# The input projection of a hybrid decoder layer as a stage of its own in seven-product form, with the scan as one chain behind it

## The chip, the cores and the metric

The kernel runs on one core of one Trainium2 chip. Its engines are PE (TensorE, matmul, with its weight loads listed as PEld), DVE (VectorE), ACT (ScalarE), POOL (GpSimd) and SP (SyncE, which here issues nearly all DMAs). The metric is the time of one execution in device microseconds; the profile records another execution, instruction by instruction.

## What is computed

One layer of a decoder on 1024 prompt tokens and 8 x 8 sample tokens, width 1024, in fp32. Cut to what matters here:

```python
x = x + 0.5 * swiglu(rmsnorm(x, norm_ffn1), ffn1_w_in, ffn1_w_out)      # D_FF = 2816
hn = rmsnorm(x, norm_mix)
proj = hn @ w_in                      # 1024 -> 8224: u 1024, z 2048, xbc 3072, dt 32, gates 2048
branch_pool = pool_mix(u) @ pool_w_out     # windowed means (2, 4, 8, 16) minus token, a 256x256 map per group
xbc_c = silu(causal_conv(xbc, width 4))    # x 2048, B 512, C 512
dt = softplus(dt_raw + dt_bias)
y = ssd_scan(x, dt, A, B, C, state) + d_skip * x       # 32 heads of 64, 4 groups, state 128, chunks of 128
y = rmsnorm_per_group(y * silu(z)) * ssd_norm
branch_ssd = y @ ssd_w_out
merged = sigmoid(g0) * branch_pool + sigmoid(g1) * branch_ssd
x = x + merged @ w_o
x = x + 0.5 * swiglu(rmsnorm(x, norm_ffn2), ffn2_w_in, ffn2_w_out)
```

The last rows before pooling and convolution and the last scan states are outputs too.

## The kernel before

The tokens stand in the free dimension, features in the partitions. They are worked in two halves: half 0 has 512 prompt tokens, half 1 the other 512 and the 64 sample tokens (`NTOK = (512, 576)`). A matmul in fp32 accuracy is three matmuls of a fast fp32 type: every operand is split into a high part (ACT) and the remainder (DVE), and `products` (L318) runs high x high, low x high, high x low. `dense` (L329) makes one output tile of 128 features for one half: 8 blocks of 128 inputs x 3 products, in half 1 as two pieces of 288 columns. `load_w` (L269) fetches a block of weights, splits it on ACT (`wh`, L292) and DVE (`wl`, L293) and, with `keep`, writes both parts to DRAM, so that half 1 reads them back instead of splitting again.

FFN1 and FFN2 use another form (`wino`, L481): the 2 x 2 block product of two token quarters, two input quarters and two output tiles is done in seven block products in place of eight. `combine` (L508) makes the sums of the activations, `wino_weights` (L442) the sums of the weights on POOL (L451) and their splits (L457, L458), and a callback `after` gathers the products from three PSUM banks. Both halves of the tokens are worked on with one loading of the weights. A few leading tiles are done in the plain form (`ffn_in_plain`) while the sums for the other half are made.

Between the FFNs stands the token mixer, `mix_half` (L1375), once for each half. It runs `mix_dt` (step sizes), `mix_pool` (u tiles, windowed sums, group map, `gate` and `pool_w_out`, L962 to L1062), then, for each of four groups, `proj_group` (L1094: six `conv_tile`s: projection `pc`, convolution on DVE at L1088, SiLU by tanh), `z_tiles` (L1381), the group's scan `ssd_group` (L1323), the gating (L1355) and `ssd_out` (L1392, `pso`), then the merge and `w_o` (`pwo`).

The scan of a group goes chunk by chunk, 4 chunks of 128 tokens and in half 1 a fifth for the samples. A chunk has a first part `ssd_a` (L1168: transposes `pxT`, `pcb`, scaled inputs, decays), a second part `ssd_b` (L1224: `pyo`, `pyd`, additions into `y4`; for the samples also the states of eight sequences, `ph0T`, `pnew`, `pyos`) and the state step `ssd_st` (L1302: `pst`, `hst`). The second part of a chunk comes after the first part of the next. The gating multiplies by z (L1359), squares, sums (`rstd`, L367, with `pss`, a power on POOL at L361, `prb`), scales and splits into `yh`, `yl` (L1364 to L1370).

What runs beside what is written by a planner in the kernel. Side work stands in `Chain`s, generators that yield a delay; the clock `pe` counts the columns of the matmuls issued so far, and after each step of a dense matmul `tick` runs the chains whose time is due. `finish` steps one chain to its end at once, whatever its due times. So instructions of the scan stand between dense matmuls in PE's order when there are such matmuls, and next to each other when a `finish` forces them. Each engine then works its own order one after the other.

Of the kernel before, what the change touches and what calls it, by code (L numbers as in the profile page):

```python
# [38 lines left out]
N_PLAIN, N_APART = (3, 2), 1  # L39

PRODUCTS = (("1", 0), ("2", 1), ("6", 0), ("5", 2), ("7", 0), ("3", 2), ("4", 0))

STEP = (6.5, 4.8)
SSD0 = (2.0, 2.0)
CONV_D = (1.0, 3.0)
STEP_S = 2.5
GP = (0.7, 1.2)
PACE = 2.0
# [9 lines left out]
PART_AT, PART_W, PART_PACE = 20.0, 4.0, 3.0  # L58
N_PRE = 3
# [3 lines left out]
def tile_hybrid_pool_ssd_macaron(  # L63
# [45 lines left out]
    def fx(dt=F32, name="x"):  # L109
        if stage["name"] == "mix":  # L110
            return act((P, 576), dt, name)
        return stage["p"].tile([P, 576], dt, tag="fx", bufs=N_FX, name=nm(name))
# [104 lines left out]
    cwh = cp.tile([P, 5, 24], F32, tag="cwh", name="cwh")  # L217
# [13 lines left out]
    def load_consts():  # L231
# [16 lines left out]
        for j in range(4):  # L248
            V.tensor_scalar_mul(cwh[:, j, :], cols[:, i_cw[j] : i_cw[j] + 24], 0.5)
        V.tensor_scalar_mul(cwh[:, 4, :], cols[:, i_cb : i_cb + 24], 0.5)  # L250
# [9 lines left out]
    dtd_sd = dp.tile([NS, NH], F32, tag="dtdsd", name="dtdsd")  # L260

# [105 lines left out]
    def rstd(tiles, h, count, out, pace=1.0):  # L367
# [4 lines left out]
        for i, x in enumerate(tiles):  # L372
            if i == 0:
                S.activation(s, x, AF.Square)
            else:
                q = act((P, N), name="sq")
                S.activation(q, x, AF.Square)
                V.tensor_tensor(s, s, q, op=ALU.add)
# [27 lines left out]

    def norm_split(xt, h, gi, out, pace=1.0):

        N = NTOK[h]
        rr = []  # L410
        yield from rstd(xt, h, D, rr, pace)
        hi, lo = [], []
        for k in range(KD):
            a, b, _ = pair(N)
            t = act((P, N), name="xn")
            V.tensor_tensor(t, xt[k], rr[0], op=ALU.mult)
            split(t, a, b, cols[:, gi + k : gi + k + 1])
            hi.append(a)
            lo.append(b)
            yield pace  # L420
        out.append((h, hi, lo))
# [217 lines left out]
    def ffn(wi, wo, prep, after, half=None, side=None):  # L639

        X, todo, behind = [{}, {}], [], []
        for h in HALVES:
# [11 lines left out]
            for ff in range(N_PLAIN[h]):  # L656
                ffn_in_plain(wi, ff, x[:3])
            todo.append(c)
            behind.append(start(rest(c, gen)))
        for c in behind:  # L660
            finish(c)
        if side:
# [133 lines left out]
    def norm_parts(xt, h, gi, out, pace=1.0):  # L796
# [5 lines left out]
        for k in range(KD):  # L802
            x = fx(name="xn") if k >= 4 else act((P, 576), name="xn")
# [6 lines left out]
            hl.append(both)  # L810
            yield pace
        out.append((h, hi, lo, xn, hl))


    ch, hn = {}, []
    wi1 = ffn1_w_in[0]

    def after1(h, xt):
        if h == 0:
            ch["hn"] = start(norm_split([t[:, : NTOK[0]] for t in xt], 0, i_gm, hn, HN_PACE), HN_AT)  # L820
        for m in range(KD):
            dma(xspill[h][m], xt[m][:, : NTOK[h]])

# [20 lines left out]
    def side():  # L844
        yield from part(ffn1_w_out[0], out01)
        yield from part(ffn2_w_in[0], [(kb, 4, c0 + ff * P) for ff in range(N_PLAIN[0]) for kb in (0, 4) for c0 in (0, FF)])
        yield from part(w_o[0], [(kb, 4, m * P) for m in range(KD) for kb in (0, 4)])

    ffn(wi1, ffn1_w_out[0], prep1, after1, side=side())
    finish(ch["hn"])  # L850
# [4 lines left out]
    W = w_in[0]  # L855
    uhist = cp.tile([P, KD, HIST], F32, tag="uhist", name="uhist")
    chist = cp.tile([P, 24, 3], F32, tag="chist", name="chist")
# [11 lines left out]
    def evac_raw(pts, h, raw, off, raws, offs):  # L869

        if h == 0:
            S.copy(raw[:, off : off + 512], pts[0][:, :512])
            return
        S.copy(raw[:, off : off + 288], pts[0][:, :288])
        S.copy(raw[:, off + 288 : off + 512], pts[1][:, :224])
        S.copy(raws[:, :, offs : offs + NT], pts[1][:, 224:288].rearrange("p (b t) -> p b t", t=NT))

    def mix_dt(h, xs, out):

        N = NTOK[h]  # L880
        nch = 4 + h
        n = nch * NH
# [729 lines left out]
```

## Time and profile before

| | us |
|---|---|
| median of 3 runs (lowest, highest) | 2930.04 (2925.57, 2930.72) |
| the profiled execution | 2926.27 |
| its span, first to last instruction | 2924.5 |
| granted clock of PE in it | 0.998 |
| start and end of the token mixer in it | 790, about 2165 |

The prediction shows lines of several views: the page (busy time by engine, the span in 40 slices, shares of the chain that ended last), groups of instructions (`line engine operation out<-in shapes xcount | busy us, mean ns of one | idle time of the engine before them, and what ended it`), the chain in order of time and the timeline (`start us, us, what`), and stretches (`from:to length, busy us (xinstructions)` of PE, PEld, DVE, ACT, POOL, then the granted clock, the share of the DMA engines and GB/s).

### The profile page before, as it was taken

The numbers are of one execution on the slowest core, as the hardware profiler recorded it, in microseconds if no ns is written. First come the engines' busy times: TensorE is split into PE (matmuls) and PEld (weight loads), VectorE is DVE, ScalarE is ACT, GpSimd is POOL, SyncE is SP. The second block draws the span as 40 slices with busy tenths as digits, with TensorE's granted clock in tenths as the row PEclk, the third lists the DMA queues.
The fourth block names the chain that finished last, engine by engine and source line by source line (L and its number), as shares of the span: only waits on it lengthen the run. The fifth ranks groups of instructions, "written<-read, shape, count | busy, mean of one in ns | idle before, by whom it ended". The sixth has DMA issues, their size and how long they took to land.

```text
span 2924.5 us, 50164 instructions
## 1 busy us (share of the span) xinstructions
PE 2873.3 (98%) x18622; PEld 2621.2 (90%) x18622; DVE 1706.2 (58%) x3172; ACT 1208.9 (41%) x2456; POOL 533.3 (18%) x642
## 2 busy tenths in 40 slices
PE   7999999999999999999999999999999999999998
PEld 6999999789988888788999989999999999987898
DVE  6665555434273897787643786867666554453432
ACT  5444444323242655443332554443233444443422
POOL 6444444000000000000000010100035444440000
PEclk9999999999999999999999999999999999999999
DMA  4575554854335878678434566556574532236652
GB/s 135 166 227 181 161 173 131 283 188 145 101 97 164 281 254 265 205 226 280 129 98 148 170 187 185 168 165 186 177 244 154 162 98 78 82 103 210 216 161 73
DMA packets 542266, 501.23 MB, mean 171 GB/s; under 512 B 36388, under 2 KB 391780, under 8 KB 542014
## 3 DMA queue, kind: packets, MB, share of 16 engines
q1 hardware_dynamic: 542006, 498.03, 54.4%
q8 instruction: 146, 2.39, 0.3%
q14 instruction: 98, 0.80, 0.1%
q10 hardware_dynamic: 16, 0.00, 0.0%
HBM read 355.94 MB, written 142.20 MB: 170 GB/s over the span
## 4 chain that ended last, share of the span: by engine, by line
PE 90%; DMA 4%; DVE 3%; ACT 1%; issue 1%; POOL 1%; SPq 0%; POOLq 0%; ACTq 0%; DVEq 0%
PE pw L164 26%; PE po L164 18%; PE pc L164 9%; PE pg L164 8%; PE pz L164 7%; PE pu L164 5%; PE pso L164 5%; PE pbp L164 3%; PE pwo L164 3%; PE pyd L164 1%; PE pst L164 1%; PE pyo L164 1%; DMA bsel<-in_bsel_dram 1%; PE pgm L164 1%; DMA hr<-hd 1%
## 5 line engine op out<-in xcount | busy, mean ns | idle before, releaser
L293 DVE TENSOR_TENSOR wl<-wraw,wh 128x512 fp32r<-128x512 f32 (+1 forms) x416 | 284.4, 685 | 409.2 <-ACT wh L292 396.0
L292 ACT ACTIVATE wh<-wraw 128x512 fp32r<-128x512 f32 (+1 forms) x416 | 257.4, 620 | 617.6 <-PE po L164 248.7
L164 PE MATMUL pw<-X,wh 128*128 128x288 f32 (+1 forms) x1416 | 353.9, 329 | 5.3 <-ACT v L574 3.5
L164 PE MATMUL pw<-X,wl 128*128 128x288 f32 (+1 forms) x936 | 268.6, 287 | 0.0
L164 PEld LDWEIGHTS pw<-X,wh 128*128 128x128 f32 x1416 | 237.6, 188 | 27.3 <-ACT v L574 4.2
L164 PE MATMUL pc<-hl,wh 128*128 128x288 f32 (+1 forms) x1152 | 256.6, 331 | 0.0
L164 PE MATMUL pw<-hl,wh 128*128 128x512 f32 x608 | 219.5, 396 | 1.1 <-DVE t L578 1.0
L458 DVE TENSOR_TENSOR wl<-s,wh 128x512 fp32r<-128x512 f32 x168 | 131.9, 785 | 144.4 <-ACT wh L457 122.8
L164 PE MATMUL po<-hh,wh 128*128 128x288 f32 (+1 forms) x800 | 210.4, 323 | 3.5 <-ACT hh L353 2.5
L164 PE MATMUL po<-hr,wh 128*128 128x288 f32 (+1 forms) x800 | 210.6, 322 | 0.1
L164 PE MATMUL po<-hh,wl 128*128 128x288 f32 (+1 forms) x800 | 210.0, 322 | 0.0
L164 PE MATMUL pg<-hl,wh 128*128 128x288 f32 (+1 forms) x864 | 201.7, 338 | 0.8 <-issue 0.8
L164 PEld LDWEIGHTS pc<-hl,wh 128*128 128x128 f32 x1152 | 184.5, 188 | 18.1 <-issue 3.5
L164 PE MATMUL pw<-hi,wh 128*128 128x288 f32 x640 | 189.1, 296 | 0.6 <-ACT t L610 0.6
L164 PE MATMUL pw<-hi,wl 128*128 128x288 f32 x640 | 188.4, 294 | 0.0
L164 PE MATMUL pw<-lo,wh 128*128 128x288 f32 x640 | 188.4, 294 | 0.0
L164 PEld LDWEIGHTS pw<-X,wl 128*128 128x128 f32 x936 | 176.5, 189 | 0.0
L164 PE MATMUL pz<-hl,wh 128*128 128x288 f32 (+1 forms) x768 | 174.4, 335 | 0.0
L164 PE MATMUL pw<-hl,wl 128*128 128x256 f32 x608 | 169.2, 278 | 0.0
L164 PE MATMUL pc<-hl,wl 128*128 128x288 f32 (+1 forms) x576 | 158.2, 328 | 0.0
L164 PEld LDWEIGHTS pg<-hl,wh 128*128 128x128 f32 x864 | 141.3, 189 | 15.7 <-issue 2.5
L458 DVE TENSOR_TENSOR wl<-wraw,wh 128x512 fp32r<-128x512 f32 x126 | 103.2, 819 | 87.5 <-ACT wh L457 81.0
(375 smaller groups left out, 6872.7 us busy)
## 6 DMA issues: line engine op xcount, KB each, us to landing
wh<-part SPq DMA_DIRECT2D x204, 256.0 KB
wl<-part SPq DMA_DIRECT2D x204, 256.0 KB
wraw<-in_ffn_w_in_dram SPq DMA_DIRECT2D x188, 256.0 KB
wraw<-in_w_in_dram SPq DMA_DIRECT2D x180, 256.0 KB
wraw<-in_ffn_w_out_dram SPq DMA_DIRECT2D x120, 256.0 KB
part<-wh SPq DMA_DIRECT2D x112, 256.0 KB
part<-wl SPq DMA_DIRECT2D x112, 256.0 KB
ab<-acsd SPq DMA_DIRECT2D x64, 256.0 KB
```

The costliest lines, as they stand in the source:

```text
L164: T.matmul(out, lhsT, rhs, start=start, stop=stop, skip_group_check=free)
L292: S.activation(wh, raw, AF.Copy)
L293: V.tensor_tensor(wl, raw, wh.bitcast(F32), op=ALU.subtract)
L458: V.tensor_tensor(wl, a, wh.bitcast(F32), op=ALU.subtract)
```

## The change

The input projection becomes a stage between FFN1 and the mixer, `in_proj`. The norm of both halves is made as for an FFN (`norm_parts`, `operands` with `combine`); the dt tile, 6 gate tiles of half 0 and 4 of half 1 are done in plain form, and everything else in pairs of output tiles, `proj_pair`, in seven-product form for both halves at once. Each finished tile goes to a work list from which a chain, `worker`, takes convolution and SiLU (`post_conv`), windowed sums and the difference (`post_u`), SiLU of z and tanh of the gates. All results go to DRAM (`convd`, `zd`, `gd`, `dhd` and `dld`, `dtp`).

```diff
+    def proj_pair(kind, ia, ib, xs):
+        while len(work) > 3:
+            poster[0].step()
...
+        wino(wino_weights(W, 0, 4, 4, c0 + ia * P, c0 + ib * P), 4, xs, after)
...
+    def in_proj(prep):
+        def plain(x):
+            dts.append(mix_dt(h, [x]))
+            for i in range(N_GATE[h]):          # (6, 4)
+                pg = dense(W, 0, KD, OFF_G0 + i * P, [x], name="pg0")[0]
...
+        for i in range(N_GATE[0], 16, 2):
+            proj_pair("g", i, i + 1, both)
+        for g in range(NG):
+            for kind, ia, ib in (("c", 16 + g, 20 + g), ("c", 4 * g, 4 * g + 1), ("c", 4 * g + 2, 4 * g + 3),
+                                 ("u", 2 * g, 2 * g + 1), ("z", 4 * g, 4 * g + 1), ("z", 4 * g + 2, 4 * g + 3)):
+                proj_pair(kind, ia, ib, both)
...
+        for i in range(N_GATE[1], N_GATE[0], 2):
+            proj_pair("g", i, i + 1, both[1:])
```

```diff
+    def post_conv(h, ct, raw, new):
+        for o, f in parts:
+            S.activation(o, f(0), AF.Identity, bias=..., scale=w[0])
+        yield POST
+        for j in range(1, 4):
+            for o, f in parts:
+                V.scalar_tensor_tensor(o, f(j), w[j], o, op0=ALU.mult, op1=ALU.add)
+            yield POST
+        S.activation(t[:, :N], t[:, :N], AF.Silu)
+        dma(convd[h][ct], t[:, :N])
```

The mixer keeps what follows the projection: `pool_branch` for both halves (group map and `pool_w_out`), then for each half `ssd_out` for the groups, `merge` and `out_proj`. The scans of all eight groups of both halves are one chain, `scan`, started at the head of the mixer, which reads a group's inputs back from DRAM one group ahead; the step between its parts is 7.0 on the planner's clock (6.5 and 4.8 before). `ssd_out` steps the chain on until its group is there and finishes the group's gating.

```diff
+    def scan():
+        for i, (h, g) in enumerate(todo):
+            nxt = fetch(*todo[i + 1]) if i + 1 < len(todo) else None
+            yield from ssd_group(h, g, *cur, dts[h])
+            yn = []
+            gated[h, g] = start(gating(h, g, cur[2], yn)), yn
+            cur = nxt
+
+    cs = start(scan())
+
+    def scanned(h, g):
+        while (h, g) not in gated:
+            cs.step()
+        finish(gated[h, g][0])
+        return gated[h, g][1][0]
...
+    for h in HALVES:
+        pool_branch(h)
+    for h in HALVES:
+        acc = [None] * KD
+        for g in range(NG - 1):
+            ssd_out(h, g, acc)
+        mhl = merge(h, acc)
...
+        x1 = out_proj(h, *mhl)
```

Within the scan and the gating, work moves from ACT and DVE to POOL: the skip product (ACT before, at L1326, for a whole group; now per chunk and in place), the last addition into the group's result (L1300), the product with z and the sums of squares. z is read from DRAM at the head of the gating.

```diff
+        G.tensor_tensor(xs4[:, :, tok], xs4[:, :, tok], Dcol[...], op=ALU.mult)
...
-            V.tensor_tensor(ysl, ysl, ea, op=ALU.add)
+            G.tensor_tensor(ysl, ysl, ea, op=ALU.add)
...
-    def gating(h, g, y4, z4, out):
+    def gating(h, g, y4, out):
+        E = V if (h, g) == (1, NG - 1) else G
+        zs = []
         for j in range(4):
-            V.scalar_tensor_tensor(y4[:, j, :N], z4[j], 0.5, y4[:, j, :N], op0=ALU.mult, op1=ALU.mult)
+            z = act((P, N), name="z")
+            dma(z, zd[h][g * 4 + j])
+            zs.append(z)
...
+        for j in range(4):
+            E.tensor_tensor(y4[:, j, :N], y4[:, j, :N], zs[j], op=ALU.mult)
...
-        yield from rstd([y4[:, j, :N] for j in range(4)], h, 512, rr, GP[0])
+        yield from rstd([y4[:, j, :N] for j in range(4)], h, 512, rr, GP[0], E)
+        while h * NG + g - 2 >= freed[0]:
+            yield 1.0
```

Smaller parts: the weights of `pool_w_out` are split ahead during FFN1, as those of `w_o` were; in the projection no weights are kept in DRAM any more, since they are loaded once for both halves; the states before pooling and convolution are written out tile pair by tile pair.

More of the change, by code (lines that the diff above doesn't have):

```diff
@@ L637, in ffn_in_plain, with operands @@
         dma(hdram[h][ff], g[:, : NTOK[h]])
[L639 to L643 removed]
+    def operands(prep, plain):
+        X, behind = [{}, {}], []
         for h in HALVES:
```

784 lines of the change are left out of this document (417 added, 367 removed).

## The prediction

> **What bounds the kernel now.** First the page: busy shares, the 40 slices, the chain that ended last.
>
> ```profile
> span 2924.5 us, 50164 instructions
> PE 2873.3 (98%) x18622; PEld 2621.2 (90%) x18622; DVE 1706.2 (58%) x3172; ACT 1208.9 (41%) x2456; POOL 533.3 (18%) x642
> ...
> PE   7999999999999999999999999999999999999998
> ...
> DVE  6665555434273897787643786867666554453432
> ...
> PE 90%; DMA 4%; DVE 3%; ACT 1%; issue 1%; POOL 1%; SPq 0%; POOLq 0%; ACTq 0%; DVEq 0%
> ```
>
> TensorE (PE) is the bound nearly everywhere, so a matmul removed is worth its own length as long as another stands ready behind it. The token mixer runs from 790 to about 2165 us; the stretches by half, and one stretch of FFN1 in seven-product form, are the next view (busy us of PE, PEld, DVE, ACT, POOL; clock; DMA share; GB/s):
>
> ```profile
> 790.20:1399.10 608.90, 607.62 (x2948) 496.73 (x2949) 438.52 (x812) 287.95 (x517) 19.23 (x59) 1.00 0.70 221
> 1399.10:2165.00 765.90, 761.26 (x6020) 733.84 (x6019) 498.22 (x1120) 300.54 (x663) 52.51 (x117) 1.00 0.55 167
> ...
> 365.00:438.00 73.00, 73.00 (x491) 68.62 (x490) 42.00 (x67) 33.72 (x70) 33.04 (x32) 1.00 0.53 171
> ```
>
> In the mixer PE stands still for 1.3 + 4.6 = 6 us in all: the scan, a chain over VectorE (DVE), ScalarE (ACT) and PE, is hidden behind projection matmuls that stand between its pieces. That cover is what the change takes away.
>
> **Part 1: projection matmuls.** The chain in order of time gives the plain prices, 24 matmuls a tile in half 0, 48 in half 1:
>
> ```profile
> 906.26 5.44 PE pbp L164 x24
> 911.70 5.44 PE pg L164 x24
> ...
> 1531.77 6.40 PE pg L164 x48
> ```
>
> The projection has 64 tiles (24 convolution, 16 z, 8 u, 16 gate) and the small dt tile. Plain remain dt, 6 gate tiles of half 0 and 4 of half 1. Removed: 58 x 5.44 + 60 x 6.40 = 699.5 us. Added: 29 pairs for both halves, each 7 products x (8 + 12) = 140 matmuls, and one pair for half 1 alone, 84. FFN1 has the same 140: 73.00 / 491 = 0.149 us each, 20.8 a pair. 29 x 20.8 + 84 x 6.40/48 = 614. **Saving 85 us**; the transposes of the states are the same in number. The weights no longer kept and reloaded and the results through DRAM are off PE; DMA is busy 0.70 and 0.55 above, so I cost them at nothing (uncovered they would show as waits for `wraw`). The norm of half 1 runs behind the seven plain tiles of half 0, 7 x 5.44 = 38 us, SiLU takes the place of tanh and a product: nothing either.
>
> **Part 2: DVE in the new stage.**
>
> ```profile
> L1088 DVE SCALAR_TENSOR_TENSOR ct<-craw,cwh,ct 128x512 f32<-128x512 f32 x144 | 107.6, 747 | 32.3 <-ACT ct L1086 31.2
> L1088 DVE SCALAR_TENSOR_TENSOR ct<-crs,cwh,ct 128x64 f32<-128x64 f32 x72 | 20.0, 278 | 0.0
> L293 DVE TENSOR_TENSOR wl<-wraw,wh 128x512 fp32r<-128x512 f32 x250 | 171.9, 688 | 166.2 <-ACT wh L292 164.2 <-PE prb L168 0.8 <-DMA ab<-acsd 0.7
> L458 DVE TENSOR_TENSOR wl<-s,wh 128x512 fp32r<-128x512 f32 x68 | 55.1, 810 | 51.4 <-ACT wh L457 48.8 <-POOL s L451 1.5 <-issue 0.5
> L578 DVE TENSOR_TENSOR t<-pw,t 128x512 f32<-128x512 f32 x18 | 12.3, 684 | 0.2
> L614 DVE TENSOR_TENSOR g<-pw,t 128x288 f32<-128x288 f32 x17 | 7.7, 452 | 6.6 <-PE pw L164 6.6
> ```
>
> A convolution pair holds 12 wide steps (9.0 us), 6 sample steps (1.7), 7 weight remainders (5.7) and seven additions from PSUM (3 x 0.68, one half as wide at an estimated 0.4, 3 x 0.45: 3.8): 20.2 of the 20.8 us that PE needs. The z pairs have only the last two (9.5), so the stage fits on average, but half of its pairs are full, and the work list lets three items lag, no more. A stall of 0 at the least; at most, some 3 us for each of 12 convolution and 4 u pairs, 48. I take 12, near the lower end, because FFN1 with the same bank rhythm has PE at 73.00 of 73.00.
>
> **Part 3: the scan without its cover.** After the change the dense work beside the scan is `pbp` and `pwo`, 16 x (5.44 + 6.40) = 189 us, as much again for `pso`, and the small `pgm`; the pool branch's part of it runs before the first `pso`, and a group's `pso` can't start before its scan and gating are done. The built order of PE shows what that leaves. From the last `pso` of one group of half 1 to the first of the next nothing dense stands there:
>
> ```
> pso:48 | pyo pyd pst pxT pcb | pyo pyd pst pxT pcb | pyo pyd pst pxT pcb px3 pb3 px3 pb3 | pyo pyd
> | 8 x (ph0T pnew) with 2 x (pyos pyT) | pyd pfin | pss prb pss | pxT pcb | pso:90 ...
> ```
>
> This stands so for (1,1), (1,2) and (1,3), from the sample's ph0T on for (1,0), from the second chunk on for (0,3), and for the last chunk's tail and the gating for (0,2). There the scan runs at the pace of DVE:
>
> ```profile
> L1218 DVE TENSOR_SCALAR ab<-ab,acs 128x128 f32<-128x128 f32 x256 | 55.9, 283 | 9.2 <-ACT ea L1216 7.9
> L1221 DVE TENSOR_TENSOR ab<-ab,cbm 128x512 f32<-128x512 f32 x64 | 43.5, 689 | 5.4 <-ACT ab L1220 4.7
> L1265 DVE SCALAR_TENSOR_TENSOR h<-h,cdp,pnew 128x128 f32<-128x128 f32 x128 | 35.7, 343 | 40.3 <-PE pnew L164 40.2
> L1203 DVE TENSOR_TENSOR xdt<-pxT,dt 128x512 f32<-128x512 f32 x32 | 22.0, 687 | 10.6 <-PE pxT L168 10.4
> ```
>
> Every 512-wide operation is 0.68 to 0.69. A chunk's first part is xdt, xd, two products with cbm, cbm itself (0.28, as one L1218) and eight L1218 at 55.9/256: 4.8. Its second part is 1.4, the state step 1.4; the product with the skip weights and the last addition move to POOL, two of 1.3 a chunk beside DVE's 7, on which only the gating waits. The forced stretch of a half-1 group holds two first parts (9.6), four second (5.5), five state operations (3.4), the sample chunk's first part (eight 512-wide and twelve small, 7.7) and second (32 L1265 at 0.28 and three small, 9.9): 36 us. Back to back they follow 0.09 closer (next rows: 0.60 from xdt to cbm), so 32 to 36; I take 34. PE's own work in it:
>
> ```profile
> 1994.54 0.69 DVE L1203 TENSOR_TENSOR xdt<-pxT,dt 128x512 f32<-128x512 f32 x1 [0.33 <-PE pxT L168]
> 1995.14 0.28 DVE L1197 TENSOR_TENSOR cbm<-pcb,tri 128x128 f32<-128x128 f32 x1
> ...
> 1999.45 1.05 PE L164 MATMUL pyo<-Cf,hst 128*128 128x128 f32 x8
> 2000.43 1.09 PE L164 MATMUL pyd<-ab,xdt 128*64 128x128 f32 x16
> ...
> 2002.02 0.83 PE L164 MATMUL pso<-yh,wh 128*128 128x288 f32 x2
> ...
> 2038.48 0.39 PE L164 MATMUL pnew<-bblk,X 96*128 96x512 f32 x1
> 2038.71 0.60 PE L168 MATMUL ph0T<-ident,h 128*128 128x128 f32 x4
> 2039.07 0.78 PE L164 MATMUL pz<-hl,wh 128*128 128x288 f32 x4
> ```
>
> 2.6 for pyo, pyd and pst together (1999.45 to 2002.02), 0.6 a sample unit (2038.48 to 2039.07): with the transposes about 24.
>
> Then the gating, in which only the next group's pxT can follow. It now loads z after the scan's end, behind the loads that SP already holds, and runs four products and three additions of 128x576 on POOL:
>
> ```profile
> 2087.66 4.04 DMA ac<-accd
> ...
> L451 POOL TENSOR_TENSOR s<-wraw,wraw 128x512 f32<-128x512 f32 x84 | 111.9, 1332 | 170.5 <-DVE wl L458 127.9 <-DMA wraw<-in_ffn_w_in_dram 40.5 <-DVE g L570 2.1
> L774 POOL TENSOR_TENSOR lo<-xn,hi 128x576 fp32r<-128x576 f32 x4 | 6.6, 1640 | 5.5 <-DVE hi L769 5.5
> L1359 DVE SCALAR_TENSOR_TENSOR y<-z,y 128x576 f32<-128x576 f32 x16 | 11.4, 756 | 0.3
> ...
> 2065.26 1.15 PE L164 MATMUL pss<-ones,ssq 128*128 128x1 f32 x10
> ...
> 2071.91 1.45 ACT L353 ACTIVATE yh<-y,cols 128x576 fp32r<-128x576 f32 x2
> ```
>
> 4.0 for the load, 7 x 1.5 = 10.5 on POOL (against 7 x 0.75 = 5.3 where DVE keeps them, the last group), and 7.4 from the start of pss to the end of the first of two yh: 22. So (1,1) and (1,2) cost 34 + 22 - 24 = 32 each; (1,3) 27; (1,0), with the sample's second part alone and 12 of PE in it, 20; (0,3), two first parts with what follows (16) and 21 of gating against 13 of PE, 24; (0,2) 2 + 21 - 5 = 18; (0,0) and (0,1), where pss stands 6 us into a chain of 4 + 9.5 with dense work behind it, 5 each. **Exposed: 163 us.** Bounds: 100, with z landed in time, POOL at 1.1 and DVE at the closer pitch; 215, with 8 more of handovers a group between PE, ACT and DVE.
>
> **Part 4: the clock.** A pause of PE leaves a mark in the granted clock:
>
> ```profile
> 30.00:40.00 10.00, 7.59 (x41) 6.10 (x41) 5.10 (x11) 3.53 (x10) 7.50 (x18) 0.95 0.23 68
> 40.00:50.00 10.00, 10.00 (x52) 8.44 (x51) 7.91 (x14) 5.21 (x14) 4.38 (x4) 0.88 0.23 57
> ...
> 2910.00:2925.00 15.00, 1.27 (x10) 0.77 (x8) 5.78 (x13) 5.14 (x14) 1.17 (x1) 0.71 0.45 157
> ```
>
> 0.05 x 10 + 0.12 x 10 = 1.7 us lost around one pause. Six restarts of dense work after an exposed gating: 10 us; 0 to 40, if the thin scan between counts as a pause as well. [...]
>
> **Sum.** On the profiled execution, 2926.27 us (span 2924.5): -85 + 12 + 163 + 10, and -6 for the idle time that the old mixer had: 2926 + 94 = 3020. The profiled execution lies 3.8 under the median of the runs, inside their spread, so **3020 us** stands for both.
>
> **Rivals.** (a) *The cover holds.* The exposed stretches are half as long or less: the engines reach the forced stretches with a good part of the scan already done, since the order is by a plan in which PE's clock alone counts. For it: POOL 18% and ACT 41% busy have room, and the first groups run behind `pbp`. Against: 36 us of DVE and 22 us of gating in one dependency chain each, whatever the room. With 75 exposed and 5 of clock: 2926 - 85 + 12 + 75 + 5 - 6 = 2927; with 40 exposed, 2890. Faster begins where the exposure falls under about 73, some 9 us for each of eight groups. (b) *DVE bounds the new stage as well.* It is the convolution pairs: 20.2 of 20.8 at prices without POOL beside them; L1088's 747 was taken with POOL idle, and the remainders with POOL busy have 810 against 688 in the mixer. Then +48 instead of 12: 3056. [...] (d) *No saving by seven products*, since weight sums on POOL and splits come late: 3020 + 85 = 3105. Against: FFN1's full 73.00.
>
> **How the numbers follow.** Forecast 0.60, (a) 0.15, (b) 0.15, (c) 0.08, (d) 0.02. (a) splits about 0.12 faster, 0.02 within 0.2% (5.9 us, as little as a measurement of this kernel tells from none), 0.01 slower. Slower in all 0.86. The range: from the 100 of part 3 (2957) a little into (a), 2948, to (b) and most of (c), 3070; below it 0.13, above it 0.06.
>
> **What would show it.** Right: an input-projection stage near 700 us (7 x 5.44 + 5 x 6.40 + 614 + 12) with PE full, and in the second half of the mixer six or seven gaps of PE, 15 to 35 us each in sum per group, ending on `rsm` (POOL) and `yhl` (ACT, DVE), with the granted clock under 0.95 there. Part 1 is wrong if a pair takes over 21.5 us; part 2 if PE waits there for `ct` or `wl` more than 30 us in all; part 3 if PE is over 95% busy from the first `pso` of half 1 on: then (a) has come, and the time is under 2930.

## The result, and the profile after

The changed kernel takes 3141.31 us (median of four runs, 3136.64 to 3142.46) against 2929.48 us before (four runs): 1.072 times, 95% interval 1.070 to 1.074. It is slower, by 212 us where 94 were forecast, and the time lies above the range. The profiled execution took 3142.46 us. Its page, the lines that answer to those of before:

```profile
span 3140.7 us, 51060 instructions
PE 2881.3 (92%) x18494; PEld 2615.7 (83%) x18494; DVE 1812.9 (58%) x3220; ACT 1269.6 (40%) x2592; POOL 1001.6 (32%) x1018
...
PE   7999996999999999999899879666789999999998
...
DVE  6555556334654868778655667455776554444432
...
PEclk9999998999999999999999889777889999999999
...
PE 66%; DVE 6%; DMA 5%; issue 3%; POOL 3%; ACT 2%; SPq 1%; POOLq 0%; ACTq 0%; DVEq 0%
```

PE is busy as long as before (2881 against 2873 us) although matmuls were taken out; it stands still in slice 7 (the end of FFN1's input stage) and in slices 23 to 30, where the granted clock drops too. The stages in stretches, first of before, then of after (busy us of PE, PEld, DVE, ACT, POOL; clock; DMA share; GB/s). The bounds are the first `pdt` and the end of the last `pwo`; after, also the end of the new stage:

```profile
0.00:790.20 790.20, 763.52 (x4896) 704.80 (x4896) 414.65 (x678) 334.13 (x695) 246.48 (x263) 1.00 0.55 173
790.20:2166.50 1376.30, 1370.38 (x8976) 1231.89 (x8976) 936.79 (x1932) 588.49 (x1179) 71.74 (x176) 1.00 0.62 191
2166.50:2924.50 758.00, 739.42 (x4752) 684.55 (x4751) 354.71 (x564) 286.25 (x582) 215.09 (x203) 0.99 0.42 135
```

```profile
0.00:817.60 817.60, 767.10 (x4896) 706.84 (x4896) 430.07 (x694) 344.36 (x720) 253.46 (x266) 0.98 0.60 187
817.60:1542.10 724.50, 708.74 (x4666) 658.29 (x4664) 525.03 (x871) 373.95 (x769) 340.01 (x390) 1.00 0.37 114
1542.10:2378.70 836.60, 662.95 (x4185) 563.58 (x4184) 505.78 (x1092) 265.10 (x523) 193.97 (x160) 0.85 0.65 208
2378.70:3140.70 762.00, 742.55 (x4751) 687.02 (x4751) 351.97 (x564) 286.19 (x582) 214.16 (x203) 0.99 0.42 134
```

So FFN1 grew by 27.4 us, the mixer by 724.5 + 836.6 - 1376.3 = 184.8, what follows by 4.0: 216 in all. The new stage has PE full (15.8 us idle in 724.5). The part behind it, called the tail from here on, has PE idle for 173.6 us of 836.6, at a mean clock of 0.85.

**FFN1.** The chain of waits around slice 7:

```profile
524.07 5.21 DMA pr<-in_pool_w_out_dram
...
536.43 3.69 DMA pr<-in_pool_w_out_dram
...
540.14 0.64 ACT ph L354
...
540.80 0.70 DVE pr L356
...
541.90 3.36 DMA pr<-in_pool_w_out_dram
...
547.03 3.92 DMA hr<-hd
```

The list of weights that are split beside FFN1's matmuls (`side()`) was not through when `finish(side)` came, and its last pieces ran one behind the other, load, split, store, about 5.5 us each, while `hr`, which the output matmuls need, stood behind them in SP's queue.

**The gating of (1,0)** in order of time (start, us, engine):

```profile
1972.74 0.72 POOL L1410 TENSOR_TENSOR xs<-xs,ea 128x256 f32<-128x256 f32 x1 [26.59 <-DVE ea L1409]
...
1974.76 1.88 SPq L1469 DMA_DIRECT2D z<-zd  x4
1980.21 4.11 POOL L1474 TENSOR_TENSOR xs<-xs,z 128x576 f32<-128x576 f32 x3 [6.75 <-DMA z<-zd]
...
1987.00 2.88 POOL L379 TENSOR_TENSOR ssq<-ssq,sq 128x576 f32<-128x576 f32 x2
...
1989.93 2.17 PE L162 MATMUL pss<-ones,ssq 128*128 128x1 f32 x10 [16.78 <-POOL ssq L379]
...
1997.24 1.33 PE L162 MATMUL pso<-yhl,wh 128*128 128x288 f32 x4 [0.48 <-ACT yhl L354]
```

From the scan's end (1973.5) to the first `pso` 23.8 us pass: 6.7 until z has landed, 9.7 of POOL, 7.3 from `pss` on. The prediction had 22.

**The gaps.** Six stretches lie between dense work and the first `pso` of (0,2), (0,3), (1,0), (1,1), (1,2), (1,3). The windows that hold them:

```profile
1774.20:1793.80 19.60, 6.37 (x43) 5.52 (x42) 4.21 (x7) 4.24 (x7) 12.20 (x10) 0.64 0.41 146
1820.90:1861.70 40.80, 19.52 (x127) 14.87 (x127) 22.37 (x47) 10.66 (x21) 18.11 (x16) 0.70 0.50 157
1953.50:1997.20 43.70, 20.61 (x151) 15.27 (x149) 12.12 (x40) 10.08 (x17) 12.58 (x11) 0.58 0.52 150
2029.20:2096.80 67.60, 36.42 (x287) 27.43 (x285) 37.39 (x97) 21.86 (x45) 21.48 (x18) 0.72 0.44 128
2128.00:2197.60 69.60, 38.41 (x287) 29.29 (x285) 37.51 (x99) 21.27 (x43) 21.47 (x17) 0.69 0.38 114
2227.80:2289.40 61.60, 35.38 (x281) 26.55 (x279) 42.71 (x107) 21.34 (x44) 10.90 (x9) 0.74 0.47 140
```

302.9 us in six gaps. No engine fills one: in the fourth DVE is busy 37.4 of 67.6, PE 36.4, at clock 0.72. PE is idle for 146.2 us of the six together and busy for 156.7.

### The profile page after: what moved, and what is told of

Same layout as the page of the kernel before. It is cut to its first block, busy times and chain, and to the rows that moved or that the text cites. A ratio compares the mean times of both kernels' runs of the same rounds, so it can differ in the third digit from the quotient of the medians.

```text
span 3140.7 us, 51060 instructions
## 1 busy us (share of the span) xinstructions
PE 2881.3 (92%) x18494; PEld 2615.7 (83%) x18494; DVE 1812.9 (58%) x3220; ACT 1269.6 (40%) x2592; POOL 1001.6 (32%) x1018
## 4 chain that ended last, share of the span: by engine, by line
PE 66%; DVE 6%; DMA 5%; issue 3%; POOL 3%; ACT 2%; SPq 1%; POOLq 0%; ACTq 0%; DVEq 0%
PE pw L162 30%; PE po L162 17%; PE pso L162 5%; PE pbp L162 2%; PE pg L162 2%; PE pwo L162 2%; PE pu L162 1%; POOL xs L1474 1%; POOL ssq L379 1%; DMA h<-in_state_ssm_dram 1%; PE pyd L162 1%; PE pst L162 1%; DMA z<-zd 1%; DMA pr<-in_pool_w_out_dram 1%; DVE us L951 1%
## 5 line engine op out<-in xcount | busy, mean ns | idle before, releaser
L162 PE MATMUL pw<-X,wh 128*128 128x288 f32 (+1 forms) x2484 | 623.3, 330 | 13.0 <-ACT v L559 3.9
L162 PE MATMUL pw<-X,wl 128*128 128x288 f32 (+1 forms) x1644 | 472.7, 288 | 1.9 <-DVE wl L443 1.9
L162 PEld LDWEIGHTS pw<-X,wh 128*128 128x128 f32 x2484 | 418.0, 189 | 52.1 <-ACT v L559 4.8
L436 POOL TENSOR_TENSOR s<-wraw,wraw 128x512 f32<-128x512 f32 x144 | 205.7, 1429 | 309.7 <-DVE wl L443 218.5
L294 DVE TENSOR_TENSOR wl<-wraw,wh 128x512 fp32r<-128x512 f32 x228 | 158.1, 695 | 251.9 <-ACT wh L293 240.3
L443 DVE TENSOR_TENSOR wl<-wraw,wh 128x512 fp32r<-128x512 f32 x216 | 166.2, 770 | 137.4 <-ACT wh L442 132.0
L162 PEld LDWEIGHTS pw<-hl,wh 128*128 128x128 f32 x1072 | 201.2, 188 | 42.0 <-DVE t L563 5.8
L162 PE MATMUL po<-hh,wh 128*128 128x288 f32 (+1 forms) x800 | 212.0, 325 | 25.5 <-ACT hh L354 25.3
L442 ACT ACTIVATE wh<-s 128x512 fp32r<-128x512 f32 x288 | 181.5, 630 | 130.9 <-PE pw L162 128.8
L162 PEld LDWEIGHTS pw<-hi,wh 128*128 128x128 f32 x1120 | 210.1, 188 | 12.2 <-DVE rb L1095 0.5
L162 PEld LDWEIGHTS pw<-lo,wh 128*128 128x128 f32 x1120 | 210.2, 188 | 0.0
L162 PEld LDWEIGHTS pw<-hi,wl 128*128 128x128 f32 x1120 | 210.1, 188 | 0.0
```

The costliest lines, as they stand in the source:

```text
L162: T.matmul(out, lhsT, rhs, start=start, stop=stop, skip_group_check=free)
L294: V.tensor_tensor(wl, raw, wh.bitcast(F32), op=ALU.subtract)
L436: G.tensor_tensor(t, a, b, op=op)
L442: S.activation(wh, a, AF.Copy)
L443: V.tensor_tensor(wl, a, wh.bitcast(F32), op=ALU.subtract)
```

## The experiments

Each run is one execution, except where an interval is given. "Tail" goes from the first `pgm` to the end of the last `pwo`. In four kernels whose edits leave it alone, but for the splits that e1_side moves into the pool branch (the changed one, e1_side, e9_plain, e14_pace), it took 829 to 841 us, so less than some 10 us of it says nothing alone. The kernel before took 2926.8 to 2932.4 beside these runs.

| run | time, us | first `pdt` | tail |
|---|---|---|---|
| changed kernel | 3141.3 | 817.6 | 835.6 |
| e1_side | 3124.0 | 793.5 | 840.5 |
| e14_pace | 3132.9 | 802.6 | 837.1 |
| e3_gatev | 3109.8 | 818.7 | 799.4 |
| e4_zearly | 3119.8 | 818.4 | 809.9 |
| e6_three | 3072.7 | 790.7 | 789.9 |
| e13_states | 3134.7 | 821.4 | 824.1 |
| e9_plain | 3154.3 | 819.4 | 828.9 |
| e2_warm | 3200.8 | 820.1 | 889.7 |
| e5_warmg | 3131.9 | 821.0 | 820.2 |
| e10_warms | 3138.6 | 818.9 | 831.3 |
| e17_gates | 3133.1 | 817.0 | 821.9 |
| e18_light | 3137.0 | 817.8 | 827.4 |
| e7_cover | 3043.1 | 818.2 | 734.8 |
| e8_all | 3003.4 | 794.4 | 712.3 |
| e11_relief | 3012.8 | 791.8 | 725.2 |
| e12_split | 3008.6 | 794.6 | 721.5 |
| e16_best2 | 2998.5 | 801.5 | 704.5 |
| e15_best | 2980.0 | 803.6 | 685.9 |

### FFN1's list of weights

```diff
-        for w in (w_o[0], pool_w_out[0]):
+        for w in (w_o[0],):
```

> pool_w_out isn't split ahead in FFN1; the pool branch splits it itself. Account of the trace: TensorE's 25.3 us gap at 525 to 551 us is the end of the list of weights to be split, worked off one load after the other while the next stage's loads stand behind it. Then the gap goes, the first pdt comes back from 817.6 to 790 us, and the kernel takes 27 us less, 3114 (3108 to 3120). Rival: the splitting only moves, and 32 splits on ScalarE and VectorE are exposed in the pool branch (1543 to 1708 us): then 3120 to 3140, and pbp waits for wl there.

The first `pdt` came 24.1 us earlier, the time fell by 17.3. The loss sits in FFN1, as the first account had it, but the time lies in the rival's range: the tail is 5 us longer, the projection stage 3. That the moved splits are the reason isn't shown: in the pool branch PE waits 0.9 us for them, and 5 us is half of the tail's own spread. e14_pace keeps the list and makes it due earlier:

```diff
-PART_AT, PART_W, PART_PACE = 20.0, 4.0, 2.5
+PART_AT, PART_W, PART_PACE = 20.0, 3.0, 1.5
```

> pool_w_out is still split ahead in FFN1, but the list is paced faster: 3.0 and 1.5 us of TensorE's work between its steps instead of 4.0 and 2.5, so that its 56 pieces are due over 252 us instead of 364. Open: whether FFN1's 27 us are the splitting's work or its lateness. Account by lateness: the list is through before the input stage of FFN1 ends, the 25 us gap goes, first pdt at 790 to 796 us, 3116 (3110 to 3124). Account by work: ScalarE, VectorE and the DMA do as much as before, and matmuls wait elsewhere in FFN1: first pdt at 805 or later, 3128 or more.

The first `pdt` came at 802.6, between the two accounts; the time is that of the second. The longest wait of `po` on `hh`, 23.1 us in the changed kernel, is 7.1 here:

```profile
PE po L162 <- ACT hh L354: 8.9, 4, 7.1
```

So 15 of the 27 us are lateness that an earlier due time cures. Of the other 12, 7 are still the same wait: the last piece is split at 530.4 us, after PE has stopped at 529.5, so this list came late too. The last 5 stay open.

### The gating's chain: POOL and the loads of z

e3_gatev sets the engine of the gating to DVE in all groups; e4_zearly loads z ahead of the last chunk; e6_three is both, with e1_side.

```diff
-        E = V if (h, g) == (1, NG - 1) else G
+        E = V
...
+        for j in range(4):
+            z = act((P, NTOK[h]), name="z")
+            dma(z, zd[h][g * 4 + j])
+            zs.append(z)
         yield step
         for w in ssd_b(h, g, *prev, Cf, y4, dts):
```

> The gating's products with z and its additions run on VectorE in all eight groups. Account: seven 128x576 operations of 1.4 us in a row on GpSimd (1980.2 to 1989.9 us in the gating of (1,0)) become seven of 0.76: 4.4 us less in each of the five exposed gatings, 22 us (15 to 30), 3120. Rival: VectorE is the pace of the scan, and what it takes over delays the next group's scan by as much: 3135 to 3150.

> The four tiles of z are loaded before the last chunk of a group's scan instead of after it. Account: in the gating of (1,0) GpSimd stands 6.75 us until z lands, and nothing else of the chain runs in that time; without it five exposed gatings are 6 us shorter each: 30 us less (20 to 35), 3112. Rival: the loads only take the place of others that the scan waits for (ab, the sample's states): less than 10 gained, 3130 to 3145.

> e1_side, e3_gatev and e4_zearly together, to see whether their gains add: 18.5 + 32.7 + 22.7 = 74 less, 3068 (3060 to 3080). Rival: z's wait and GpSimd's products lie one behind the other only by chance, and with both shortened another wait (the sample's loads, ScalarE's squares) ends last: 3080 to 3100.

e3_gatev: 31.5 us less, just over the upper end of its account. The five gaps that had POOL fell by 4.2, 4.6, 5.7, 5.1 and 4.6 us (24 together), the sixth, where DVE already did it, by 0.1; of the other 7, 4 are a wait for POOL in the gating of (0,1), between dense matmuls, which is gone, and the rest is inside the spread. In the changed kernel it stands here:

```profile
1714.71 1.87 PE L162 MATMUL pss<-ones,ssq 128*128 128x1 f32 x8 [4.07 <-POOL ssq L379]
```

DVE has the room there, so the rival falls. e4_zearly: 21.5 less, gaps 0, 2.2, 7.7, 3.7, 7.7 and 4.9 shorter (26). Together, with e1_side: 68.6 less where the single runs sum to 17.3 + 31.5 + 21.5 = 70.3. They add: in the gating the waits follow each other, and each is worth its length.

### The gaps in the scan: loads or handovers

```diff
-            h0s = {0: load(units[0]), 1: load(units[1])}
+            h0s = {u: load(units[u]) for u in range(4)}
```

> The sample's states are loaded four units ahead instead of two; nothing else. Open: between the pso of one group of half 1 and the next lie 61 to 70 us, 12 more than forecast, while VectorE is busy 37 of them. Account 1: part of it is TensorE's wait for the states (ph0T from DMA, 12.1 us in 9 waits): those waits go, the gaps are 3 us shorter each, 3130 (3126 to 3136). Account 2: the surplus is handovers between TensorE, ScalarE and VectorE, the loads only end last by chance: the gaps stay within 1 us, 3138 to 3146.

The waits of PE in the tail of the changed kernel (us in total, times, longest):

```profile
PE pss L162 <- POOL ssq L379: 67.3, 6, 16.9
PE pss L162 <- POOL rsm L390: 13.5, 1, 13.5
PE ph0T L166 <- DMA h<-in_state_ssm_dram: 12.1, 9, 2.3
...
PE pcb L162 <- DVE ea L1408: 8.6, 4, 3.9
PE px L166 <- ACT xr L1257: 8.1, 3, 3.2
PE pgm L162 <- DMA d<-dl: 8.1, 2, 7.8
PE pyT L166 <- ACT yt L1386: 5.7, 8, 0.8
```

In e13_states the third is 1.6 us, and the gaps of (1,1), (1,2), (1,3) fell by 0.4, 6.0 and 5.3; the time by 6.7. In the four kernels that leave these gaps alone they scatter by 2 to 3 us; against the means of the four the falls are 0.8, 4.6 and 3.7. So the loads were some 9 to 12 us of the surplus, near the first account's 3 a gap, on one execution.

Where most of the rest lies is seen in the gap of (1,0), which has nothing but the sample's second part and the gating in it. The stretch up to the scan's end, and pieces of the chain that ended last there:

```profile
1953.50:1973.50 20.00, 15.35 (x129) 10.96 (x127) 10.31 (x36) 5.60 (x10) 0.72 (x1) 0.67 0.82 239
```

```profile
1950.98 4.92 DMA h<-in_state_ssm_dram
...
1956.93 1.06 PE pyos L162 x32
...
1958.01 0.59 ACT yt L1386
...
1959.34 0.30 DVE ea L1393
...
1959.88 4.54 DMA h<-in_state_ssm_dram
...
1967.36 1.91 PE pyos L162 x32
```

It takes 20.0 us. The prediction had 9.9, DVE's own work, and DVE is in fact busy for 10.3; but in the chain DVE stands for 0.3 us, PE for 10.6, the loads of the states for 6.9 and ACT for 1.5. In (1,1), (1,2) and (1,3) the same part takes 16.0, 18.9 and 19.1 us from its first `ph0T` to the scan's end. So it holds 34 of the 48 us that the six gaps are over the forecast: 74 us in the four groups where 40 were priced (67 to 72 in e1_side, e9_plain and e14_pace). With the states loaded earlier (e13_states) it is 60, and with more clock (e18_light, below) 65; how the rest divides into slow matmuls and handovers between engines was not separated.

### Seven products or plain

```diff
-N_GATE = (6, 4)
+N_GATE = (16, 16)
```

> All 32 gate tiles in plain form, so five pairs for both halves and one for half 1 alone become 10 x 24 and 12 x 48 plain matmuls; all else of the changed kernel stands. Account of the prediction's part 1: 10 x 5.44 + 12 x 6.40 = 131.2 us in place of 5 x 21.2 + 12.7 = 118.7 (628.6 us for 4144 matmuls in the changed kernel): 12 more, 3154 (3148 to 3162), so a saving of 2.5 us a pair. Rival: the pairs save nothing on the chip, their waits eat it: 3138 to 3146. Second rival: plain tiles save even waits on GpSimd's weight sums: under 3138.

From the first `pdt` to the first `pgm` 740.9 us passed instead of 725.5; the kernel took 13.0 more. In the stage the plain tiles cost 193.55 - 62.29 = 131.3 us more and the pairs 628.62 - 515.35 = 113.3 less: 18 us saved by six pairs (one of them for half 1 alone), some 3 a full one. The saving is there.

```profile
817.60:1542.10 724.50, 628.62 (x4144) 584.55 (x4144) 111.31 (x206) 105.53 (x235) 1.00 0.37 114
```

(The changed kernel's `pw` alone in the new stage: 4144 matmuls, 628.62 us, 0.1517 each, 21.2 a pair.)

### The clock

Idle matmuls on the constant `ones` are put where PE waits; they write into a bank that the next real matmul starts anew.

```diff
         pt = psum("ps", "pss")
+        if warm:
+            fill(pt, 60)
...
+        if (h, g) in ((1, 1), (1, 2), (1, 3)):
+            fill(py, 8)
```

> TensorE runs idle matmuls of the constant ones into a bank that the next real matmul overwrites: 60 ahead of pss and 20 ahead of prb in the gatings of (0,2), (0,3), (1,0), (1,1), (1,2), and 8 in each scan step and sample unit of (1,1), (1,2), (1,3); nothing else changes. Account by the clock: the granted clock falls to 0.50 when TensorE stands still for some us and stays there some 10 us into the dense pso behind it; filled, it stays near 1.0, pso, pwo and the scan's own matmuls lose their 82 us of extra length in part: 25 us less from the pso behind five gaps, up to 60 less with the scan steps, so 3080 to 3115. Rival: VectorE and GpSimd set the pace of the thin stretches, the slow matmuls there lie under them: at most 10 less, 3130 to 3150. Second rival: the clock falls for another reason than the gaps: still under 0.9 in 1700 to 2300 us, and time the same or more.

It took 60 us more, outside every account: 60 such matmuls ahead of `pss` took 13.56 us, 0.226 each, so 8 are an estimated 1.8, in the scan longer than the waits that they were to fill, and each of the three groups has 18 such places. It shows only that the clock was higher with PE kept busy (mean 0.978 against 0.952). In windows of 2 us of the changed kernel it is back at 1.00 some 5 to 8 us behind the start of `pso`, where the account has 10. The next two were sized by the 0.226 us. e5_warmg has 68 ahead of `pss`, 6 ahead of `prb` and none in the scan; e10_warms adds more, among them these:

```diff
+        if (h, g) in ((1, 0), (1, 1), (1, 2), (1, 3)):
+            fill(py, 3)
...
         yn = scanned(h, g)
+        if (h, g) in ((0, 2), (0, 3), (1, 0), (1, 1), (1, 2)):
+            fill(psum("ps", "pfl"), 12)
```

> The idle matmuls of e2_warm only where TensorE waits anyway: 68 ahead of pss (0.226 us each in e2_warm, 15.4 us against waits of up to 16.9) and 6 ahead of prb, in the same five gatings; none in the scan. Account by the clock: pso behind a gating then starts at full clock; in the trace of the changed kernel it ran 10 us at 0.50 to 0.76, so some 4 to 6 us less at each of the five, 20 to 30 in all: 3112 to 3122. Rival: what follows the gap is set by ScalarE and VectorE (yh and yl), not by the clock: 3135 to 3150.

> Idle matmuls in all the thin parts, kept short: 68 ahead of pss, 6 ahead of prb and 12 ahead of the first pso in the five gatings, 3 ahead of pyd, 3 ahead of pxT and 2 ahead of pnew in the scans of (1,0) to (1,3). Account by the clock: e5_warmg left 0.67 to 0.84 between prb and the first 8 us of pso; filled through, the granted clock stays over 0.95 from 1700 to 2350 us, and the slow matmuls that lie on the path give back their share: 25 to 50 less than the changed kernel, 3092 to 3118. Rival: VectorE is the pace of the scan, and the 42 us of filling there delay it: clock up, time 3130 to 3180.

e5_warmg gained 9.4 us, less than half of what the account said, and e10_warms 2.7, though the tail's mean clock rose from 0.85 to 0.94 and 0.96. Two more, with four executions each, look closer: of e10_warms' fillings e17_gates leaves out the scan's (and has 74 ahead of `pss`), and e18_light makes them `fill(py, 2)` and `fill(px, 2)`:

> What a pause costs by the clock, alone: idle matmuls in the five gatings only, 74 ahead of pss, 6 ahead of prb and 12 ahead of the first pso, none in the scan. Account: the first 8 us of pso run at full clock in all five, 4 us each, 15 to 20 less than the changed kernel, 3121 to 3127. Rival: ScalarE and VectorE set the pace of the first pso, and the clock costs nothing there: 3136 to 3142.

> e17_gates with 2 idle matmuls (0.45 us) ahead of pyd and of pxT in the scans of (1,0) to (1,3), 18 us of them in all, none ahead of pnew. Account: the scan between two pso runs at the pace of VectorE and of handovers, not of the clock: the granted clock goes up there and the gaps stay, within 6 of e17_gates. Rival: the slow matmuls are links of the chain; at full clock each gap is 5 to 8 us shorter: 20 to 30 less than e17_gates.

e17_gates: 3133.1 us, 1.0694 times the kernel before (1.0678 to 1.0710). e18_light: 3137.0, 1.0709 (1.0691 to 1.0727). e17_gates falls between its accounts. It is 8 us under the changed kernel (its interval just touches that one's 1.0704 to 1.0741, the times themselves don't overlap), and `pso` in all takes 209.2 us instead of 220.7. So the pauses cost at least some 8 us by the clock. They cost more by what the filling itself adds: in the gap of (0,2) the 74 outlast the wait, `pss` starts 18.4 us into the gap instead of 13.1, and the gap is 4 us longer. Filling the scan as well brings nothing more; its last three gaps stay at 67.8, 65.4 and 58.8 us. So e18_light speaks for its first account. Its matmuls in the scan are faster: of the twelve `pyd` of 16 ahead of the samples in (1,1), (1,2) and (1,3) eleven take 1.09 us and one 1.36, where four take 1.50 to 1.98 in the changed kernel. The four scans of half 1 take 146 us, against 148 in e17_gates and 148 to 154 in the kernels that leave them alone. In the chain that ended last the idle matmuls ahead of `pyd` and `pxT` stand for 0.4 to 2.2 us a gap, so a few us a gap that the slow matmuls cost could be hidden by that.

### Cover

e7_cover changes the order alone: smaller steps of the scan, and the pool branch of half 1 behind half 0.

```diff
-STEP = (7.0, 7.0)
+STEP = (4.0, 4.0)
...
     for h in HALVES:
         pool_branch(h)
-    for h in HALVES:
         acc = [None] * KD
...
+            while i > 1 and not gated[todo[i - 2]][0].done:
+                yield 1.0
             nxt = fetch(*todo[i + 1]) if i + 1 < len(todo) else None
```

> Only the order is changed: a scan step is due after 4.0 us of TensorE's work instead of 7.0, the pool branch of half 1 (64 us of dense matmuls) moves from ahead of the first pso to ahead of half 1's, and a group's loads wait until the gating two groups before is issued. By the order that is then built no pso stands less than a whole scan step behind its scan. Account by cover: the exposed scan (171 us of TensorE idle from 1543 us on) and the clock's loss with it (82 us) mostly go: about 645 us of matmuls at full clock plus 12 at the pool branch's start plus 30 of handovers against 897: 200 less, 2940 (2920 to 2990). Rival: VectorE, 546 us busy in that part, can't keep up when everything stands side by side, and the scan itself takes longer: half of it, 3040 (3000 to 3080).

98 us less: the largest single effect of all runs, and nearly half of the 212 that were lost. So much of the loss is missing cover, and it is the planner's order and not the arithmetic that leaves the scan bare; which of the two edits did how much was not tried. But it is half of what was expected; the rival's 3040 is met to 3 us.

> e7_cover with e1_side, e3_gatev and e4_zearly. Account by cover: with the gatings hidden z and GpSimd no longer count, and only FFN1's 20 to 24 us come off e7_cover: 2916 (2895 to 2970), under the kernel before if e7_cover is under 2950. Rival: the gating is still what a pso waits for, and the three give their 74: e7_cover less 74.

3003.4, so neither account holds: it is 40 us under e7_cover, 24 of them from FFN1, and the tail is 22 shorter. With cover the gating still counts, but for less than half of the 53 us that e3_gatev and e4_zearly brought. What stands in the way is looked for in e8_all's windows (the tail begins at 1524.5):

```profile
1570.00:1670.00 100.00, 91.18 (x524) 69.45 (x524) 92.14 (x193) 51.36 (x103) 22.24 (x17) 0.97 0.68 216
1670.00:1770.00 100.00, 86.01 (x482) 62.57 (x481) 91.48 (x194) 46.09 (x93) 21.36 (x19) 0.98 0.70 228
...
2120.00:2237.00 117.00, 113.36 (x877) 110.39 (x875) 83.79 (x141) 31.03 (x50) 29.19 (x25) 1.00 0.77 256
```

While half 0 is scanned, DVE is busy 92 of 100 us and PE 91 and 86; at the end PE is full (113 of 117) and DVE has room. DVE as the bound there is a reading of these shares, which the next runs try. The four that follow shift work off DVE, and PE's work forward (the first diff is e11_relief's, the second e12_split's):

```diff
-                V.tensor_tensor(hn_.rearrange(
+                G.tensor_tensor(hn_.rearrange(
...
-            V.tensor_tensor(t1[m], t1[m], acc[m], op=ALU.add)
+            (V if h else G).tensor_tensor(t1[m], t1[m], acc[m], op=ALU.add)
```

```diff
         for g in range(NG - 1):
+            if (h, g) == (0, 2):
+                pool_branch(1)
             ssd_out(h, g, acc)
```

> e8_all with work taken off VectorE: the gating's products with z and its additions back on GpSimd (but for the last group), the state's product with the decay and half 0's last addition of the merge on GpSimd too: 24 + 17 + 7 us of the 302 that VectorE was busy in 1545 to 1895 us. Account: with cover VectorE is the bound of that part (22 to 25 of each 25 us busy, TensorE 21): 30 less than e8_all (15 to 45), 2973. Rival: each GpSimd operation takes 1.3 to 1.5 us in place of 0.7 to 0.86 and two of them lie in the chain of the scan: the same or up to 20 more, 3000 to 3025.

> e11_relief with the pool branch of half 1 between the second and the third pso of half 0 instead of after half 0. Account: TensorE has more to do while VectorE is full, and less is left for the end, where in e8_all TensorE is full and VectorE half idle (2095 to 2295 us): 20 to 30 less than e11_relief, 2948 (2930 to 2975). Rival: the last groups' scan loses its cover and is exposed again: 0 to 30 more than e11_relief.

Both accounts missed. e11_relief is 9 us slower than e8_all, as its rival has it, though that is inside the spread: with the gating on POOL, `pss` stands in PE's queue for 35.6 us on POOL's `ssq`, for its due time (1.5 us of PE's work after the last addition) was made for a faster chain, and all dense work stands behind it. e12_split gains 4 on it, inside the spread. e15_best therefore makes `pss` due later, splits `pool_w_out` in FFN1 at e14_pace's pace, and loads states and the pool branch's input earlier; e16_best2 is the same with the gating and the state's product on DVE.

```diff
-        yield max(pace, 1.5)
+        yield 7.0 if E is G else max(pace, 1.5)
...
-        for k in range(2):
+        for k in range(4):
             ahead_d.append(load_d(0, k))
```

> e11_relief with pool_w_out split ahead at e14_pace's pace, four states ahead, four of the pool branch's inputs loaded ahead instead of two, and pss due 7 us instead of 1.5 after a gating's last addition on GpSimd. Account: with cover a wait of TensorE's queue is worth its length: pss's 36 us and the 10 us at the pool branch's start go, 22 us of splits come off VectorE: 40 to 60 less than e11_relief, 2955 to 2972. Rival: VectorE bounds the part whatever its order: 2985 to 3005.

> As e15_best, but with the gating and the state's product on VectorE as in e8_all. Account by VectorE as bound: 22 us of splits off VectorE and 10 us at the pool branch's start: 25 less than e8_all, 2978 (2965 to 2990), and above e15_best. Rival: GpSimd's longer operations cost more than VectorE's load: under e15_best.

e15_best: 2980.0, 33 under e11_relief, between its two accounts; PE's wait at `pss` is 9.6 us instead of 35.6. e16_best2 is 18 above it, as its account by DVE as bound has it, but it gained only 5 on e8_all where 25 were expected. That points to DVE's load counting once the wait in PE's queue is gone; several edits differ, so it isn't shown singly. e15_best is the fastest form of the changed kernel found here, 161 us under it, and still 53 over the kernel before (2927.2 in the same set of runs). No version was faster than the kernel before.

## Why the prediction was wrong

The direction, the stage, the seven products and the bare gaps came as forecast; the size didn't. Two steps failed: the scan's length, taken from DVE's own work, and FFN1, which had no term at all. Point by point, with the difference to the forecast where there is one:

- **Part 1, 85 saved.** Right by its own measure: a pair takes 21.2 us, under 21.5. But FFN1's 0.149 us a matmul was 0.1517 here: 628.6 instead of 614, +14.6. The plain tiles and dt took 62.3 + 12.2 = 74.5 instead of 70.1, +4.4. The stage took 724.5 where 696 was written (5.6 of the rest are transposes and other small matmuls that both kernels have).
- **FFN1, no term.** The sentence "The weights no longer kept and reloaded and the results through DRAM are off PE ... so I cost them at nothing" looks at DMA's share in the mixer alone, and the sum has no term for the splits of `pool_w_out`, which moved from the mixer to a place beside FFN1. The list there ran out of time: **+27.4**, of which e1_side gives back 24.1. DMA's mean share was the wrong view: what mattered was the due times of the list (56 pieces at 6.5 us of PE's work, 364 us) against the length of the stage that hides it.
- **Part 2, 12 for DVE.** Right: PE is idle 15.8 us in the stage, +4; rival (b) falls.
- **Part 3, 163 exposed.** The place and the mechanism are right, the lengths short. By the terms of the prediction the six gaps are 23, 37, 32, 56, 56 and 51 us, 255 with PE's own work in them; they measured 302.9, +48. The groups (0,0) and (0,1), priced at 5 each, waited 1.5 and 4.1 us at `pss`, so **+44** net. The gating was well priced (23.8 against 22). The scan was not: the 34 of "at the pace of DVE" is about 43 in the fourth gap (67.6 less 24), near the 8 of handovers a group that stood as the upper bound. The term that was mis-sized most is the sample chunk's second part, 9.9, which took 16.0 to 20.0 in the four groups that have it; the two gaps of half 0, which have none, came at 60.4 where 60 were written. DVE wasn't the pace: it is busy 37 of 67.6 us with the gating's part in it. A chain that goes from engine to engine has the sum of its links for its length, loads among them, and the busiest engine's share is only the least that it can be. That PE's idle time in the gaps, 146, came out near the 153 of the prediction is luck: the surplus shows as PE's own matmuls, 156.7 where 102 were written.
- **Part 4, 10 for the clock.** Six restarts were right in kind: the dense matmuls take 31 us more than before (`pso` 220.7 for 207.8, `pbp` 103.5 for 96.3, `pgm` 29.1 for 25.3, `pwo` 103.6 for 96.0). But `pbp` and `pgm` stand mostly ahead of the six gaps, so their part has another reason, and e17_gates returns 8 of the 31 in time, at least. The chance (c), a clock that stays low in the thin stretches, had the direction right: it was at 0.58 to 0.74 in every gap. Its part in the upper end of 3070 was the author's estimate, with PE at half pace through a group's whole scan, which no run shows. The three last gaps are 11 to 14 us over the forecast, but with their clock raised from 0.72, 0.69 and 0.74 to 0.93, 0.95 and 0.84 (e10_warms) they took 69.7, 67.0 and 60.9 us instead of 67.6, 69.6 and 61.6, so the surplus isn't shown to be the clock's.
- **Not in the sum**: the pool branch's first groups wait 10 us for `d` (8.1 and 2.2 in the waits), and what follows the mixer is 4 longer.
- **Rival (a), the cover holds**, fell (its sum for 40 exposed is 2892, not 2890). e7_cover shows what it would have needed: an order that lets the scan run ahead, which the built order of PE, read before, plainly lacked.

The misses sum, with each as above: 27.4 + 4.0 + 14.6 + 4.4 + 4 + 44 + 10 = 108 of the 122 us between 216 and 94; the remaining 14 lie in the dense stretches of the tail, where the matmuls take 31 more and 10 were forecast. The range failed because these misses all fall on the same side, most of them places where work costed as hidden stood bare, and the upper end of 3070 took in one of them at a time.

## What to carry to other kernels

If a change gathers dense matmuls in a stage of their own, price what they hid as the length of the whole dependent chain, link by link with its loads and handovers, and check by the built order how far ahead that chain can run. Work moved into "free" time of another stage must be held against that stage's length in the planner's own units: here the last pieces of a late list ran one after the other, about 5.5 us each, in front of the next stage's loads, and FFN1 took 27.4 us longer. A wait on POOL cost PE much or little by when the instruction that waits came into PE's queue: 35.6 us of waits at `pss`, due after 1.5, in e11_relief, 9.6, due after 7.0, in e15_best (which has other edits beside).

## What the hardware showed that was not expected

In the changed kernel the granted clock fell after shorter pauses than the one in part 4, and stayed low while PE worked. In part 4's rows PE stood still for 2.03 us, up to 36.2; windows of the kernel before behind that pause:

```profile
36.00:38.00 2.00, 1.81 (x16) 1.84 (x16) 0.69 (x2) 0.00 (x0) 1.68 (x7) 1.00 0.03 8
38.00:40.00 2.00, 2.00 (x12) 1.78 (x12) 0.28 (x1) 0.89 (x2) 0.00 (x0) 0.74 0.69 197
40.00:42.00 2.00, 2.00 (x6) 1.57 (x5) 1.38 (x3) 0.76 (x3) 0.00 (x0) 0.50 0.00 0
42.00:44.00 2.00, 2.00 (x13) 1.78 (x13) 1.54 (x4) 1.23 (x3) 1.10 (x1) 0.91 0.27 66
44.00:46.00 2.00, 2.00 (x14) 1.68 (x13) 1.68 (x3) 1.10 (x4) 0.86 (x2) 1.00 0.71 197
```

Windows of the changed kernel in the scan's end and behind the gating of (1,0), and two waits of PE there:

```profile
1958.00:1960.00 2.00, 0.66 (x4) 0.43 (x4) 0.67 (x3) 0.59 (x1) 0.00 (x0) 1.00 1.12 334
1960.00:1962.00 2.00, 1.28 (x5) 1.03 (x5) 0.00 (x0) 0.10 (x1) 0.00 (x0) 0.62 1.12 327
1962.00:1964.00 2.00, 1.75 (x6) 1.04 (x5) 1.32 (x5) 1.07 (x2) 0.00 (x0) 0.50 0.93 272
...
2000.00:2002.00 2.00, 2.00 (x10) 2.00 (x10) 1.61 (x4) 0.56 (x1) 0.00 (x0) 0.50 0.00 0
2002.00:2004.00 2.00, 2.00 (x10) 2.00 (x9) 1.75 (x3) 0.37 (x2) 0.00 (x0) 0.50 0.00 0
2004.00:2006.00 2.00, 2.00 (x14) 2.00 (x13) 0.27 (x1) 0.00 (x0) 0.00 (x0) 0.78 0.54 147
```

```profile
1960.72 1.08 PE L166 MATMUL ph0T<-ident,h 128*128 128x128 f32 x4 [1.42 <-DMA h<-in_state_ssm_dram]
...
1999.34 0.85 PE L162 MATMUL pso<-yhl,wh 128*128 128x288 f32 x2 [0.77 <-DVE yhl L358]
```

The clock fell to 0.50 after a stretch of 2 us with PE busy for a third of it; the longest pause near it was the 1.42 us shown. Stretches busy for 64 to 88%, and single ones of 2 us busy throughout (1966 to 1968), did not bring it back. PE then worked without a break from 1999.3, and the 0.78 of the last window puts the return at about 2004.9, 5.5 us later; reckoned the same way it came at about 42.4 in before, 6.2 us behind the end of the pause. What a clock of 0.50 costs in a stretch that other engines pace stays open within a few us a gap: with the clock of the three last gaps at 0.84 to 0.95 (e10_warms) they stayed within 3 us, but the filling itself stood in the path.
